# Two transformer blocks on one core: fp32 dispatch activations with one more weight tile, and another order of splits, scales and attention units around the sparse index

## The chip, the cores and the metric

The kernel runs on one core of a Trainium2 chip. Its time is that of one execution on the device, in microseconds (us); the median of several runs is compared. Engines are named as the profile names them: PE (TensorE matmul), DVE (VectorE), ACT (ScalarE), POOL (GpSimd) and SP (SyncE, which issues the weight transfers). Each engine works through its own instructions in program order and waits at semaphores for the others.

## What is computed

All is fp32, for 256 tokens of width 1024 (batch 1). The first block has convolution and neighbourhood attention, then 16 experts of which each chooses its own 32 tokens. The second has a sparse attention (top 64 keys of each query by an index score), an MLP, a latent attention and a second MLP.

```python
def ec_moe(h, w_router, w_gate, w_up, w_down):      # 16 experts, D_EXPERT 2048
    cap = EC_FACTOR * T // N_EXPERTS                # 32 tokens for each expert
    aff = softmax(h @ w_router)
    wts, tok = lax.top_k(swapaxes(aff, 1, 2), cap)
    xs = h[bidx, tok]                               # the dispatch
    hid = silu(xs @ w_gate) * (xs @ w_up)
    y = (hid @ w_down) * wts
    return zeros_like(h).at[bidx, tok].add(y)

def dsa_mixer(h, w_in, q_gain, k_gain, w_o, rel_bias, n_top):
    q, k, v, qi, ki, wi = split(h @ w_in)           # 16 query heads, one key/value head, 8 index heads
    q, k = rms_norm_2(q, q_gain), rms_norm_2(k, k_gain)
    score = sum_h(wi * relu(qi . ki))               # masked to admissible keys
    _, idx = lax.top_k(score, n_top)
    logits = q . k[idx] * A_HEAD_DIM ** -0.5 + rel_bias[t5_bucket(idx - t)]
    return softmax(logits) @ v[idx] @ w_o

x = first_block(x, ...)                             # ends in ec_moe
h = x + dsa_mixer(rms_norm_2(x)); h = h + sq_relu_mlp(rms_norm_2(h))
h = h + mla_mixer(rms_norm_2(h)); return h + sq_relu_mlp(rms_norm_2(h))
```

## The kernel before

**Weights** come in one fixed list (`loads`), issued on SP in that order. `pump` issues the next as soon as the buffer that the list names for it is free, and stops at the first that isn't; `take` and `free` follow the list on the consuming side. Expert weights use buffers of 2 MB, and for expert 0 some extra places (`RSA`, `RSB`, `RPW`, `RPN`, `RB`, `RC`) in memory that the stages before have left. `w_gu` of an expert is eight pieces of 2 MB (k = 0 to 7), `w_dn` four of 2 MB, which `parts` cuts differently for expert 0.

**Dispatch.** After wout, the normalized tokens are transposed back to token rows by ACT (`htk_out`), as a rounded half and, by POOL, the rest (`htk`, fp32r). DVE finds each expert's 32 tokens (L1008 to L1014) and PE gathers them by matmuls with a one-hot matrix (`disp`): `gather0` for expert 0, a chunk at a time between its `gate_up` steps, and `gather(g)`, twice, for the others.

**Splits.** From the second block on a product of fp32 matrices is three fp32r products, of rounded halves (`wh`, `xgh`) and remainders (`wl`, `xgl`). So each weight of 1 MB is split ahead of its use: ACT writes `wh` (L330), then DVE (L334) or POOL (L332) subtracts; `on_dve` says which. `wahead(k)` makes splits until k exist, `wnext(la)` takes one and makes `la` more. Splits 0 to 3 are the key, value and index weights (`kvi`), 4 to 7 the four query projections (`qproj(0)` to `qproj(3)`), 8 to 11 the four slots of the output projection (`dsawo`).

**The index.** After `kvi`, PE sums squares into a bank (`sps`), and DVE makes the inverse roots (`rsq`, eight small operations) of the block's norms in SBUF tiles. PE broadcasts them (`rb_`); `index_mm`, `index_acc` and `index_top` (eight rounds of MAX8 and MATCH_REPLACE8, then the mask `msk`) give the top 64 for query half 1 (256 keys) and half 0 (128 keys). `qscale(g)` makes the scales `rq` of the projected queries two projections at a time.

**The attention** has eight units (query half, group of 4 heads). `pipeline` runs it by step i: scores S(i+2), finish of unit i-2 (DVE, two operations that make hi and lo halves of the result), reciprocals and normalization of unit i (DVE, POOL), softmax of unit i+1 (DVE scales and finds the maximum, ACT exponentiates), then what `pre` lists for i, PV(i-1), the transposes T(i), and what `hooks` lists for i. Half 1 makes large units (256 keys), half 0 small ones. `qproj(3)` and `index_top(0)` (`itop`) are hooks of step -1. Slot u of dsawo needs both units of head group u and split 8 + u.

Of the kernel before, what the change touches and what calls it, by code (L numbers as in the profile page):

```python
# [63 lines left out]
def kernel(ctx: ExitStack, tc: tile.TileContext, *aps):  # L64
# [154 lines left out]
    inuse = [0] * 10  # L219
    lim = [R1, R2] + [0] * 8  # L220
    ps_ = []

    def buf(r):
        return pools[r].tile([P, 2048 if r in (RB, RC, RPN) else W1], F32, tag="w", name=nm("w"))
# [1860 lines left out]
```

## Time and profile before

| what | value |
|---|---|
| median of three runs | 1748.01 us (1747.1 to 1751.78) |
| the profiled execution | 1741.9 us, its span 1740.1 us |
| busy PE, DVE, ACT, POOL | 1356.5, 542.5, 426.0, 271.8 us of the span |
| transfers | 545.85 MB, mean 314 GB/s |
| the chain that ended last | 52% transfers, 38% PE, 5% DVE, 3% ACT |

A busy share is a mean over stages with different limits. The chain is followed back from the last instruction, at each step to what released it. Times within the kernel are counted from the start of the span.

### The profile page before, as it was taken

What the parts mean: (1) busy time and instruction counts of PE and PEld (TensorE: products, weight loads), DVE (VectorE), ACT (ScalarE), POOL (GpSimd) and SP (SyncE); (2) the same over time, 40 slices, a digit from 0 to 9 for tenths busy, and PEclk for the clock granted to TensorE, in tenths of its full rate; (3) what the DMA queues carried; (4) which work ended last, traced back from release to release, by engine and by line L of the source; (5) the groups of instructions that cost most, each with busy time, mean ns of one, the idle gap of its engine ahead of it and who ended that gap; (6) DMA issues with size and microseconds to landing.
All of it is one profiled execution on the core that took longest, in us unless ns stands there. A gap on an engine that the chain in (4) does not pass through costs nothing.

```text
span 1740.1 us, 22284 instructions
## 1 busy us (share of the span) xinstructions
PE 1356.5 (78%) x9581; PEld 873.8 (50%) x9581; DVE 542.5 (31%) x1037; ACT 426.0 (24%) x649; POOL 271.8 (16%) x124
## 2 busy tenths in 40 slices
PE   6899987666666655665666656798999999999998
PEld 3775842111111111221111111385899999889998
DVE  3885321000000000000000000278653457756434
ACT  3434510000000000000000000254554446455442
POOL 2521210000000000000000000152335221323531
PEclk9999999868778878878788787798999999999999
DMA  9649779999999999999999999972255544225450
GB/s 397 240 156 417 290 326 429 427 428 428 427 428 428 427 428 427 427 429 427 428 427 428 428 428 428 399 287 97 97 194 194 194 174 154 97 98 194 178 201 34
DMA packets 59475, 545.85 MB, mean 314 GB/s; under 512 B 5552, under 2 KB 9008, under 8 KB 26032
## 3 DMA queue, kind: packets, MB, share of 16 engines
q1 hardware_dynamic: 56400, 537.71, 74.9%
q10 hardware_dynamic: 2976, 6.72, 1.1%
q8 instruction: 75, 1.23, 0.3%
q14 instruction: 24, 0.20, 0.0%
HBM read 543.36 MB, written 1.05 MB: 313 GB/s over the span
## 4 chain that ended last, share of the span: by engine, by line
DMA 52%; PE 38%; DVE 5%; ACT 3%; issue 2%; POOL 1%; ACTq 0%; SPq 0%; DVEq 0%; POOLq 0%
DMA moe__w<-in_w_gu_dram 32%; DMA moe__w<-in_w_dn_dram 15%; PE mlp__psB L94 10%; PE mlp__psA L94 9%; PE index__psA L94 2%; DMA moe__w<-in_w_dl_dram 2%; PE mlaproj__psA L94 1%; PE mlawo__psA L94 1%; PE qkv__psA L94 1%; PE qkv__psB L94 1%; PE uproj__psA L94 1%; PE moe__psB L94 1%; DMA na__nb<-in_nab_dram 1%; PE router__psB L94 1%; PE wout__psA L94 1%
## 5 line engine op out<-in xcount | busy, mean ns | idle before, releaser
L94 PE MATMUL moe__psB<-moe__w,moe__xsT 128*32 128x512 f32 x1920 | 304.0, 767 | 191.7 <-DMA moe__w<-in_w_gu_dram 191.6
L94 PEld LDWEIGHTS moe__psB<-moe__w,moe__xsT 128*32 128x32 f32 x1920 | 58.9, 126 | 422.9 <-DMA moe__w<-in_w_gu_dram 312.3
L94 PE MATMUL moe__psB<-moe__w,moe__hT 128*32 128x512 f32 (+1 forms) x984 | 167.5, 808 | 103.1 <-DMA moe__w<-in_w_dn_dram 94.1
L1134 DVE TENSOR_TENSOR moe__hid<-moe__hid,moe__psB 128x512 f32<-128x512 f32 x15 | 10.3, 687 | 555.8 <-PE moe__psB L94 555.8
L332 POOL TENSOR_TENSOR dsaproj__wl<-moe__w,dsaproj__wh 128x1680 fp32r<-128x1680 f32 (+1 forms) x5 | 19.7, 3945 | 908.9 <-ACT dsaproj__wh L330 902.2
L94 PEld LDWEIGHTS moe__psB<-moe__w,moe__hT 128*32 128x32 f32 x984 | 38.4, 133 | 214.9 <-DMA moe__w<-in_w_dn_dram 139.7
L94 PE MATMUL mlp__psA<-mlp__hh,mlp__wl 128*128 128x256 f32 x512 | 141.3, 276 | 0.0
L94 PE MATMUL mlp__psA<-mlp__hh,mlp__wh 128*128 128x256 f32 x512 | 141.3, 276 | 0.0
L94 PE MATMUL mlp__psA<-mlp__hl,mlp__wh 128*128 128x256 f32 x512 | 141.3, 276 | 0.0
L1133 ACT ACTIVATE moe__hid<-moe__psB 128x512 f32<-128x512 f32 x15 | 9.0, 597 | 537.8 <-PE moe__psB L94 537.8
L94 PE MATMUL mlp__psB<-mlp__xgh,mlp__wh 128*128 128x256 f32 x448 | 123.8, 276 | 0.0
L94 PE MATMUL mlp__psB<-mlp__xgh,mlp__wl 128*128 128x256 f32 x448 | 123.7, 276 | 0.0
L94 PE MATMUL mlp__psB<-mlp__xgl,mlp__wh 128*128 128x256 f32 x448 | 123.7, 276 | 0.0
L330 ACT ACTIVATE mlp__wh<-mlp__w 128x2048 fp32r<-128x2048 f32 (+1 forms) x51 | 96.8, 1900 | 62.3 <-PE mlp__psA L94 48.6
L334 DVE TENSOR_TENSOR mlp__wl<-mlp__w,mlp__wh 128x2048 fp32r<-128x2048 f32 (+1 forms) x35 | 84.7, 2420 | 80.1 <-ACT mlp__wh L330 80.1
L332 POOL TENSOR_TENSOR mlp__wl<-mlp__w,mlp__wh 128x2048 fp32r<-128x2048 f32 x16 | 74.4, 4648 | 147.5 <-ACT mlp__wh L330 147.5
L94 PEld LDWEIGHTS mlp__psA<-mlp__hh,mlp__wh 128*128 128x128 f32 x512 | 96.1, 188 | 0.0
L94 PEld LDWEIGHTS mlp__psA<-mlp__hl,mlp__wh 128*128 128x128 f32 x512 | 96.1, 188 | 0.0
L94 PEld LDWEIGHTS mlp__psA<-mlp__hh,mlp__wl 128*128 128x128 f32 x512 | 96.1, 188 | 0.0
L1169 DVE COPY moe__ys<-moe__psB 128x512 f32<-128x512 f32 x15 | 10.4, 691 | 243.7 <-PE moe__psB L94 243.7
L94 PEld LDWEIGHTS mlp__psB<-mlp__xgh,mlp__wl 128*128 128x128 f32 x448 | 84.1, 188 | 0.0
L94 PEld LDWEIGHTS mlp__psB<-mlp__xgl,mlp__wh 128*128 128x128 f32 x448 | 84.1, 188 | 0.0
(602 smaller groups left out, 2508.2 us busy)
## 6 DMA issues: line engine op xcount, KB each, us to landing
moe__w<-in_w_gu_dram SPq DMA_DIRECT2D x120, 2048.0 KB, 39.1
moe__w<-in_w_dn_dram SPq DMA_DIRECT2D x57, 2048.0 KB, 39.1
mlp__w<-in_mlp_down_dram SPq DMA_DIRECT2D x28, 1024.0 KB, 7.0
mlp__w<-in_mlp_up_dram SPq DMA_DIRECT2D x20, 1024.0 KB, 4.9
qkv__w<-in_w_mod_dram SPq DMA_DIRECT2D x12, 1024.0 KB, 7.0
start__w<-in_w_mod_dram SPq DMA_DIRECT2D x8, 1024.0 KB, 13.5
mod__w<-in_w_gu_dram SPq DMA_DIRECT2D x4, 2048.0 KB, 20.8
wout__w<-in_w_gu_dram SPq DMA_DIRECT2D x4, 2048.0 KB, 8.4
```

Of the source, the lines that this page charges most:

```text
L94: nc.tensor.matmul(o, lhsT, rhs, start=start, stop=stop, skip_group_check=True)
L330: nc.scalar.activation(h[:, 0:n], f, AF.Copy)
L332: nc.gpsimd.tensor_tensor(out=l[:, 0:n], in0=f, in1=h[:, 0:n].bitcast(F32), op=ALU.subtract)
L334: nc.vector.tensor_tensor(out=l[:, 0:n], in0=f, in1=h[:, 0:n].bitcast(F32), op=ALU.subtract)
L1133: nc.scalar.activation(hid, gp, AF.Silu)
L1134: nc.vector.tensor_mul(hid, hid, up)
L1169: nc.vector.tensor_copy(ys[1], yp[1])
```

## The change

It has five parts. (1) `htk` is one fp32 tile; `gather0` and `gather` do two fp32 matmuls for a chunk where they did four fp32r ones. (2) The memory that this frees holds one more weight tile of 1 MB (`RX`): expert 0's k = 7 comes as two halves in `RB` and `RX`, and its `w_dn` is cut into five parts instead of six. (3) A new `rsq_p` keeps scales in PSUM banks. (4) Splits 7 and 9 go from POOL to DVE; 5 to 9 are made at other places of the program, 8 and 9 as `pre` of steps 2 and 3 of the attention. (5) Unit (1,3) comes before (0,0) and (0,1), `itop` is a hook of step 1, and the softmax scales the scores in their own bank.

```diff
-    parts = {0: (2, 2, 4, 2, 2, 4)}
+    parts = {0: (4, 2, 2, 4, 4)}
     for e in range(NE):
         for k in range(8):
+            if e == 0 and k == 7:
+                for h2 in range(2):
+                    ld(1, I["w_gu"][e, k * P:(k + 1) * P, 2048 * h2:2048 * h2 + 2048], 2048, ring=(RB, RX)[h2], solo=True)
+                continue
...
+    def rsq_p(pool_, v, n, tag, ps):
+        r, r1, out_ = (small(pool_, n, tag + k) for k in "012")
+        t = small(pool_, n, "rq_t")
+        a, b = ps[:, 0:n], ps[:, n:2 * n]
+        nc.vector.tensor_scalar(r.bitcast(I32), v.bitcast(I32), -0.5, 1597463007.0, ALU.mult, ALU.add)
+        nc.vector.tensor_tensor(out=a, in0=v, in1=r, op=ALU.mult)
+        nc.vector.tensor_tensor(out=t, in0=a, in1=r, op=ALU.mult)
+        nc.vector.scalar_tensor_tensor(out=b, in0=t, scalar=-10.0 / 3.0, in1=t, op0=ALU.add, op1=ALU.mult)
+        nc.vector.scalar_tensor_tensor(out=r1, in0=b, scalar=5.0, in1=r, op0=ALU.add, op1=ALU.mult)
...
-                nc.scalar.activation(htk[g][:, :, t, :], bv, AF.Copy, scale=r2[:, t:t + 1])
-                bc_ = pd.tile([P, 4, P], F32, tag="hb", name=nm("hb"), bufs=2)
-                nc.scalar.activation(bc_, bv, AF.Copy, scale=r2[:, t:t + 1])
-                nc.gpsimd.tensor_tensor(out=htk[g][:, :, 2 + t, :], in0=bc_, in1=htk[g][:, :, t, :].bitcast(F32),
-                                        op=ALU.subtract)
+                nc.scalar.activation(htk[:, 4 * g:4 * g + 4, t, :], bv, AF.Copy, scale=r2[:, t:t + 1])
...
-                    for n in range(4):
-                        mm(bs[c], htk[g][:, c, n, :], disp[n % 2], n == 0, n == 3)
+                    for n in range(2):
+                        mm(bs[c], htk[:, 4 * g + c, n, :], disp[n], n == 0, n == 1)
...
-        on_dve = {5, 8, 10, 11} | {n for n in range(12, 90) if n % 3 or 43 < n < 54}
+        on_dve = {5, 7, 8, 9, 10, 11} | {n for n in range(12, 90) if n % 3 or 43 < n < 54}
...
-                w = wnext(2 if s == 3 else 0)
+                w = wnext(1 if s == 3 else 0)
...
-        v1, pv, iv1, v2c, ep, ipv = (cols[:, 2 * i:2 * i + 2] for i in range(6))
+        v1, iv1, ep = (cols[:, 2 * i:2 * i + 2] for i in range(3))
+        vr = sps[:, 32:36]
+        vp1, pv, v2c, ipv = (sps[:, 32 + 2 * i:34 + 2 * i] for i in range(4))
...
         def qproj(u):
-            w = wnext()
+            w = wnext(0)
...
-        rk = rsq(pa, vk, 2, "rk")
-        scs[1] = index_acc(1, rl1)
+        rk = rsq_p(pa, vk, 2, "rk", kst[:, 16:20])
+        wahead(6)
+        scs[1] = index_acc(1, rl1, rb_)
...
         qproj(0)
+        wahead(7)
         index_top(1, scs[1])
...
-        scs[0] = index_acc(0, rl0)
+        scs[0] = index_acc(0, rl0, r12b)
+        wahead(8)
...
-        wahead(10)
...
+                psv = pss[par][:, 0:2 * nk].rearrange("p (a k) -> p a k", a=2)
...
-                    nc.vector.scalar_tensor_tensor(out=s[:, a, 0:nk], in0=pss[par][:, a * nk:(a + 1) * nk],
-                                                   scalar=rq[:, qt, hd:hd + 1], in1=bm[:, 2 * par + a, :],
-                                                   op0=ALU.mult, op1=ALU.add)
+                    nc.vector.scalar_tensor_tensor(out=psv[:, a, :], in0=psv[:, a, :], scalar=rq[:, qt, hd:hd + 1],
+                                                   in1=bm[:, 2 * par + a, :], op0=ALU.mult, op1=ALU.add)
...
-                  [(1, 0), (1, 1), (1, 2), (0, 0), (0, 1), (1, 3), (0, 2), (0, 3)])
+                  [(1, 0), (1, 1), (1, 2), (1, 3), (0, 0), (0, 1), (0, 2), (0, 3)])
...
-        pipeline(att, 8, "dsaatt", {-2: [lambda: qscale(0, pb)], -1: [q_last, itop], 0: [q_last2], 8: [wo.slot(2, (1,))]},
-                 {6: [wo.slot(0), x3(range(0, 3))], 7: [wo.slot(1), x3(range(3, 6))],
+        pipeline(att, 8, "dsaatt", {-2: [lambda: qscale(0, pb)], -1: [q_last], 0: [q_last2], 1: [itop], 8: [wo.slot(2, (1,))]},
+                 {2: [lambda: wahead(9)], 3: [lambda: wahead(10)], 6: [wo.slot(0), x3(range(0, 3))], 7: [wo.slot(1), x3(range(3, 6))],
```

In the text "split n" counts from 0. Three places of the program show how instructions move. The first is SP's list around the router, before (128x4096 is 2 MB, 128x2048 is 1 MB; `moe__w` is first issued when expert 0 gives a buffer back):

```order
L241 DMA wout__w_1772<-in_w_gu_dram 128x4096
L241 DMA wout__w_1774<-in_w_gu_dram 128x4096
L241 DMA wout__w_1776<-in_w_dn_dram 128x2048
L241 DMA router__w_1917<-in_w_dn_dram 128x2048
L241 DMA router__w_1919<-in_w_dn_dram 128x4096
L241 DMA router__w_1921<-in_w_dn_dram 128x2048
L241 DMA moe__w_2038<-in_w_dn_dram 128x2048
L241 DMA moe__w_2053<-in_w_dn_dram 128x4096
```

and of the change:

```order
L246 DMA wout__w_1772<-in_w_gu_dram 128x4096
L246 DMA wout__w_1774<-in_w_gu_dram 128x2048
L246 DMA router__w_1918<-in_w_gu_dram 128x2048
L246 DMA router__w_1920<-in_w_dn_dram 128x4096
L246 DMA router__w_1922<-in_w_dn_dram 128x2048
L246 DMA router__w_1924<-in_w_dn_dram 128x2048
L246 DMA router__w_1926<-in_w_dn_dram 128x4096
L246 DMA moe__w_2023<-in_w_dn_dram 128x4096
```

The two halves of `w_gu` for k = 7 now go to `RB` and to the new place, and a `w_dn` tile of 2 MB (`router__w_1926`) leaves ahead of the stop at `moe__w`: from `wout__w_1772` on 10 MB instead of 9.

The second is DVE ahead of the index, before (`moe__sqa` is the last sum of squares of the first block's result, `wl_4779` split 5, L288 and L289 the begin of `rsq`, L295 its end):

```order
L315 TENSOR_TENSOR moe__sqa_4457<-moe__sqa_4457,dsaproj__sq_4749 128x256
L334 TENSOR_TENSOR dsaproj__wl_4779<-moe__w_4522,dsaproj__wh_4778 128x2048
L1311 TENSOR_SCALAR dsaproj__cols_4835<-dsaproj__psA_4773 128x2
L1312 RECIPROCAL dsaproj__cols_4835<-dsaproj__cols_4835 128x2
L1313 TENSOR_TENSOR dsaproj__cols_4835<-dsaproj__psA_4773,dsaproj__cols_4835 128x2
...
L288 TENSOR_SCALAR dsaproj__rr_4866<-dsaproj__cols_4835 128x4
L289 TENSOR_TENSOR dsaproj__rq_t_4867<-dsaproj__rr_4866 128x4
...
L295 SCALAR_TENSOR_TENSOR dsaproj__rr_4866<-dsaproj__rq_t_4867,dsaproj__rr_4866 128x4
```

and of the change (L307 is the begin of `rsq_p`, L310 the operation with one SBUF tile as both inputs, `psA_4728` the bank `sps`, `wl_4880` split 5):

```order
L334 TENSOR_TENSOR moe__sqa_4412<-moe__sqa_4412,dsaproj__sq_4704 128x256
L1332 TENSOR_SCALAR dsaproj__cols_4783<-dsaproj__psA_4728 128x2
L1333 RECIPROCAL dsaproj__cols_4783<-dsaproj__cols_4783 128x2
L1334 TENSOR_SCALAR dsaproj__psA_4728<-dsaproj__psA_4728 128x2
L1335 TENSOR_TENSOR dsaproj__psA_4728<-dsaproj__psA_4728,dsaproj__cols_4783 128x2
...
L307 TENSOR_SCALAR dsaproj__rr_4814<-dsaproj__psA_4728 128x4
...
L310 SCALAR_TENSOR_TENSOR dsaproj__psA_4728<-dsaproj__rq_t_4817 128x4
...
L1343 TENSOR_SCALAR dsaproj__wsc_4828<-dsaproj__psA_4728 128x2
...
L314 SCALAR_TENSOR_TENSOR index__rk_4869<-index__psA_4853,index__rk_4868 128x2
L353 TENSOR_TENSOR index__wl_4880<-moe__w_4477,index__wh_4879 128x2048
```

Split 5 goes from ahead of the scales to behind the key's scale, and most of the scales' operands are in the bank.

The third is DVE in the attention, before, from the end of soft(0) to the begin of soft(1) (`sc_5032` holds the index scores of half 0, `msk_4844` is their mask):

```order
L1482 TENSOR_REDUCE dsaatt__nmx_5217<-dsaatt__ss_5216 128x2
L1395 MEMSET index__sc_5032 64x64
L1398 MAX index__m_5287<-index__sc_5032 128x8
L1399 MATCH_REPLACE index__sc_5032<-index__m_5287,index__sc_5032 128x128
...
L1400 TENSOR_SCALAR dsaproj__msk_4844<-index__sc_5032 128x128
L1254 RECIPROCAL dsaatt__sm_5210<-dsaatt__sm_5210 128x2
L1254 RECIPROCAL dsaatt__sm_5218<-dsaatt__sm_5218 128x2
L1479 SCALAR_TENSOR_TENSOR dsaatt__ss_5317<-dsaatt__psA_5200,dsaproj__rq_4840,dsaproj__t_4836 128x256 x2
```

and of the change, from the end of soft(2) to split 8 (`msk_4791` is the mask of half 0, `wl_5396` split 8):

```order
L1507 TENSOR_REDUCE dsaatt__nmx_5320<-dsaatt__psA_5236 128x2
L1417 MEMSET index__sc_4991 64x64
L1420 MAX index__m_5347<-index__sc_4991 128x8
L1421 MATCH_REPLACE index__sc_4991<-index__m_5347,index__sc_4991 128x128
...
L1422 TENSOR_SCALAR dsaproj__msk_4791<-index__sc_4991 128x128
L365 CAST index__mixah_5233<-dsaatt__psB_5327 128x2x128
L1505 SCALAR_TENSOR_TENSOR dsaatt__psA_5299<-dsaatt__psA_5299,dsaproj__rq_4788,dsaproj__t_4784 128x256 x2
L1507 TENSOR_REDUCE dsaatt__nmx_5380<-dsaatt__psA_5299 128x2
L1505 SCALAR_TENSOR_TENSOR dsaatt__psA_5300<-dsaatt__psA_5300,dsaproj__rq_4788,dsaproj__t_4784 128x256 x2
L1507 TENSOR_REDUCE dsaatt__nmx_5388<-dsaatt__psA_5300 128x2
L353 TENSOR_TENSOR dsaatt__wl_5396<-dsaproj__w_4663,dsaatt__wh_5395 128x2048
```

The eight rounds go from behind soft(0) to behind soft(2), and split 8 stands behind soft(3).

## Rows read from the trace of the kernel before

**Rows 1.** The chain that ended last, by engine and by line (the page).

```profile
DMA 52%; PE 38%; DVE 5%; ACT 3%; issue 2%; POOL 1%; ACTq 0%; SPq 0%; DVEq 0%; POOLq 0%
DMA moe__w<-in_w_gu_dram 32%; DMA moe__w<-in_w_dn_dram 15%; PE mlp__psB L94 10%; PE mlp__psA L94 9%; PE index__psA L94 2%; DMA moe__w<-in_w_dl_dram 2%; PE mlaproj__psA L94 1%; PE mlawo__psA L94 1%; PE qkv__psA L94 1%; PE qkv__psB L94 1%; PE uproj__psA L94 1%; PE moe__psB L94 1%; DMA na__nb<-in_nab_dram 1%; PE router__psB L94 1%; PE wout__psA L94 1%
```

**Rows 2.** Windows of four stretches, all engines and transfers.

```profile
core 0: us, PE busy (x) PEld busy (x) DVE busy (x) ACT busy (x) POOL busy (x), PEclk, DMA share, GB/s
221.00:229.00 8.00, 5.17 (x26) 2.87 (x26) 3.08 (x11) 0.67 (x2) 2.72 (x4) 0.57 0.04 17
241.00:300.00 59.00, 46.70 (x344) 19.87 (x336) 7.31 (x15) 5.49 (x8) 0.00 (x0) 0.97 1.01 428
1205.00:1224.00 19.00, 15.67 (x101) 10.04 (x97) 16.63 (x54) 12.55 (x45) 8.48 (x10) 0.86 0.00 1
1224.00:1250.00 26.00, 25.80 (x211) 23.68 (x210) 15.26 (x29) 11.49 (x18) 9.11 (x5) 0.97 0.22 82
```

**Rows 3.** When SP issued transfers (start us, us, what, count).

```profile
208.85 1.81 SPq L241 DMA_DIRECT2D router__w<-in_w_dn_dram  x3
229.48 2.72 SPq L241 DMA_DIRECT2D moe__w<-in_w_dn_dram  x2
```

**Rows 4.** Timeline of DVE and POOL at the end of the router.

```profile
222.58 0.66 DVE L1014 CAST router__idf<-router__idu 16x32 f32<-16x32 uint32 x1
...
218.28 4.92 POOL L979 TENSOR_TENSOR router__htk<-router__hb,router__htk 128x512 fp32r<-128x512 f32 x4 [0.45 <-ACT router__hb L978]
```

**Rows 5.** PE's gathers and gate_up, and the expert transfers' landing (the page).

```profile
258.67 3.92 PE L94 MATMUL router__psA<-router__disp,router__htk 128*128 128x512 f32 x16
...
280.58 1.92 PE L94 MATMUL moe__psB<-moe__w,moe__xsT 128*32 128x512 f32 x16 [0.22 <-DMA moe__w<-in_w_gu_dram]
...
moe__w<-in_w_gu_dram SPq DMA_DIRECT2D x120, 2048.0 KB, 39.1
```

**Rows 6.** POOL, DVE and PE ahead of the index.

```profile
1147.92 4.58 POOL L332 TENSOR_TENSOR dsaproj__wl<-moe__w,dsaproj__wh 128x2048 fp32r<-128x2048 f32 x1 [3.44 <-PE dsaproj__psB L94]
...
1149.68 4.97 DVE L334 TENSOR_TENSOR dsaproj__wl<-moe__w,dsaproj__wh 128x2048 fp32r<-128x2048 f32 x1 [3.18 <-ACT dsaproj__wh L330]
...
1154.95 0.16 DVE L1313 TENSOR_TENSOR dsaproj__cols<-dsaproj__psA,dsaproj__cols 128x2 f32<-128x2 f32 x1
...
1157.14 2.00 PE L94 MATMUL index__psA<-cst,dsaproj__rr 128*128 128x128 f32 x8 [3.52 <-DVE dsaproj__rr L295]
```

**Rows 7.** The chain of waits from the index on (start us, us, what).

```profile
1160.98 5.67 PE index__psA L94 x48
...
1182.70 4.38 DVE dsaatt__rqq L288
...
1189.81 8.05 PE index__psA L94 x48
...
1224.28 6.11 PE dsawo__psA L94 x48
```

**Rows 8.** Timeline of POOL and DVE in the index.

```profile
1169.83 4.59 POOL L332 TENSOR_TENSOR index__wl<-dsaproj__w,index__wh 128x2048 fp32r<-128x2048 f32 x1 [0.84 <-ACT index__wh L330]
1182.54 4.51 POOL L332 TENSOR_TENSOR index__wl<-dsaproj__w,index__wh 128x2048 fp32r<-128x2048 f32 x1 [8.12 <-ACT index__wh L330]
...
1172.62 1.95 DVE L1400 TENSOR_SCALAR dsaproj__msk<-index__sc 128x256 fp32r<-128x256 f32 x1
```

**Rows 9.** Window of one pair of exponentials on ACT.

```profile
1190.41:1191.51 1.10, 1.10 (x7) 1.10 (x7) 1.07 (x3) 1.09 (x4) 0.00 (x0) 0.50 1.03 417
```

**Rows 10.** Windows of itop, of soft(2), of a small unit's finish and softmax.

```profile
1191.84:1197.95 6.11, 6.11 (x42) 5.91 (x41) 5.53 (x29) 1.15 (x5) 0.00 (x0) 0.76 0.35 142
1205.27:1208.59 3.32, 1.56 (x12) 1.16 (x14) 3.25 (x10) 1.09 (x4) 2.04 (x2) 0.98 0.00 0
1212.16:1215.10 2.94, 2.94 (x22) 1.96 (x24) 2.84 (x10) 2.62 (x10) 1.18 (x2) 1.00 0.02 6
```

**Rows 11.** DVE's half of split 10, after its wait.

```profile
1229.45 2.29 DVE L334 TENSOR_TENSOR dsawo__wl<-dsaproj__w,dsawo__wh 128x2048 fp32r<-128x2048 f32 x1 [3.09 <-ACT dsawo__wh L330]
```

More of the change, by code (lines that the diff above doesn't have):

```diff
@@ L218 @@
             slots.append(r)
[L219 to L220 removed]
+    inuse = [0] * 11
+    lim = [R1, R2] + [0] * 9
     ps_ = []
     def buf(r):
[L224 removed]
+        return pools[r].tile([P, 2048 if r in (RB, RC, RPN, RX) else W1], F32, tag="xs0" if r == RX else "w",
+                             name=nm("w"))
     bufs_ = {}
@@ L296, in rsq @@
         return r
+    def rsq_p(pool_, v, n, tag, ps):
[7 more added lines that the diff above has]
+        nc.vector.scalar_tensor_tensor(out=r1, in0=b, scalar=5.0, in1=r, op0=ALU.add, op1=ALU.mult)
+        nc.vector.scalar_tensor_tensor(out=a, in0=v, scalar=-27.0 / 1024.0, in1=r1, op0=ALU.mult, op1=ALU.mult)
+        nc.vector.tensor_tensor(out=b, in0=a, in1=r1, op=ALU.mult)
+        nc.vector.scalar_tensor_tensor(out=out_, in0=b, scalar=0.5625, in1=r1, op0=ALU.add, op1=ALU.mult)
+        return out_
     def sumsq(pool_, ps, src, n, c, rhs, first, last, w=1, o=0, sqb=3):
@@ L959 @@
         p2 = p2s.enter_context(pool("p2"))
-        htk = [p2.tile([P, 4, 4, P], F32R, tag=f"xs{g}", name=nm("htk"), bufs=1) for g in range(2)]
+        pools[RX] = p2
+        lim[RX] = 1
+        pump()
+        htk = p2.tile([P, 8, 2, P], F32, tag="xs1", name=nm("htk"), bufs=1)
         xsT = []
@@ L1050, in gather @@
                 for c in range(4):
-                    for n in range(4):
-                        mm(bs[c], htk[g][:, c, n, :], disp[n % 2], n == 0, n == 3)
+                    for n in range(2):
+                        mm(bs[c], htk[:, 4 * g + c, n, :], disp[n], n == 0, n == 1)
                 return bs
@@ L1066, in gate_up @@
                 xs = xsT[k // 4][:, k % 4, e * CAP:(e + 1) * CAP] if e else xs0[k]
-                w = take()
+                two = e == 0 and k == 7
                 for i, o in enumerate(gu):
+                    if i == 0 or two:
+                        w = take()
+                    w_ = w if two else w[:, 2048 * i:2048 * i + 2048]
                     for j in range(4):
-                        mm(o[32 * j:32 * j + 32, :], xs, w[:, 2048 * i + j * 512:2048 * i + (j + 1) * 512], k == 0,
-                           k == 7)
-                free()
+                        mm(o[32 * j:32 * j + 32, :], xs, w_[:, j * 512:(j + 1) * 512], k == 0, k == 7)
+                    if i or two:
+                        free()
             gu0 = (bank("B"), bank("B"))
@@ L1312 @@
         nc.vector.reciprocal(iv1, v1)
+        nc.vector.tensor_scalar(vp1, sps[:, 0:2], 1.0 / D, EPS, ALU.mult, ALU.add)
         nc.vector.tensor_tensor(out=v2c, in0=sps[:, 2:4], in1=iv1, op=ALU.mult)
@@ L1354, in qscale @@
                 nc.tensor.transpose(qc[:, t * 8:(t + 1) * 8], rw[:, t * P:(t + 1) * P], ident[0:8, 0:8])
-            vq = small(pool_, 16, "vq")
+            vq = qc[:, 32:48]
             for t in range(2):
```

27 lines of the change are left out of this document (13 added, 14 removed).

## Prediction

> **What bounds the kernel now.** I read the chain that ended last first [rows 1]: transfers hold 52% of it, nearly all of that expert weights (32% and 15%), so the first block ends when its last weights land and PE follows; the rest is PE, the two MLPs above all. The windows [rows 2] show the hole in the expert stream: from 221 to 229 the queues move 17 GB/s, from 241 on 428 GB/s, with PE at 46.70 of 59 us. The issues [rows 3] say why: the last transfer ahead of the hole leaves at 210.66 (three of them, 208.85 + 1.81), the next at 229.48, when expert 0's first matmuls give a buffer back. A byte moved into the hole is a byte less at the end.
>
> Around the sparse index PE leads the chain [rows 6, 7], with two stops: 3.52 us before the broadcast of the scales, and the stretch in which DVE's first operation of the q scale takes 4.38 us. In the attention the chain passes between DVE, ACT and PE from unit to unit, until dsawo's first slot starts on PE at 1224.28; from there PE is busy 25.80 of 26.00 us [rows 2], up to mlp0.
>
> The sum is made in this execution's time (1741.9 us, its span 1740.1). The median of the three runs shown is 1748.01, 6.1 higher, which I add at the end.
>
> **Dispatch and the extra tile.** One tile of 1.049 MB more leaves ahead of the hole and is missing behind it: 1.049 / 0.428 = 2.45 us. The 7 MB (7.34 in decimal) issued from about 209 on need 7.34 / 0.428 = 17.2 us, to about 226.5; that is before 229.5, so they fit. The extra tile waits for the memory that mix leaves when wout's matmuls end, near 209; only transfers stand behind it on SP, and a bubble there is taken out of the hole. Four POOL subtractions go, the last of which ends at 223.20 (218.28 + 4.92); DVE's cast of the chosen indices, for which PE waits, ends right behind it, after 0.66 us for 16x32 elements [rows 4]. DVE's small operations without POOL took 0.16 to 0.2 [rows 6], so I take 0.45. The transfer that restarts the stream is 2 MB instead of 1 MB, so the queue doesn't run dry once more before the second: 0.3. Together **-3.2 us**. Bounds: 0, if the tile comes late or the stream is held later, and -4.
>
> What could hold it later is the gather in plain fp32. Its 16 instructions took 3.92 us [rows 5]. The nearest fp32 row is gate_up, 16 instructions in 1.92 us with four column groups side by side: 4 x 1.92 = 7.7 us for a gather, +3.8 us, twice. Before, PE waits for a weight transfer again at 280.58; until then it works off tiles that had landed, 1.92 us each against 2.097 / 0.428 = 4.9 us of transfer. So it is level two or three tiles later than before, and the queues stay fed as long as buffers come back in time: a transfer is issued a median of 39.1 us before it lands [rows 5]. I cost it at nothing; without that cover it is up to 3 us.
>
> **Scales and splits ahead of the index.** Before, DVE does split 5 first [rows 6]: it starts at 1149.68, is held by POOL's split (1147.92 + 4.58 = 1152.50) and ends at 1154.65; thirteen small operations later, 0.19 us each, PE starts the broadcast at 1157.14 and needs 2.00 us for 8 matmuls. After, split 5 stands behind that chain, which begins when the sums are there, near 1149.5. Nine operations lead to 1151.3. The tenth (L310 of the new code) reads one SBUF tile twice while POOL is in its split; I let it wait until 1152.5. It, four more and the three that read the broadcast's bank make 8 x 0.2: PE starts near 1154.1. As it stood 0.6 us instead of 3.52, I expect the full clock: 0.96 us for the broadcast, 1.0 for the index matmuls behind it. qproj(0) starts at 1156.1 instead of 1161.0 [rows 7], **-4.9**.
>
> Two rules of the Trainium skill bear on this, and the sum needs neither. "SBUF — State Buffer", section "Who interferes with whom": a DVE operation with at most one SBUF input, outside the two-port modes, does not contend with GpSimd; one with two SBUF inputs contends with GpSimd's reads. The trace agrees in split 5 (4.97 us beside POOL, 2.29 without it [rows 6, 11]); by this rule the tenth operation waits, without it the broadcast comes 0.9 us sooner. "Perfetto Trace Analysis", section "Optimizing Scalar/DVE Operations", speaks against the change: about 125 ns of access overhead for DVE on PSUM, 60 on SBUF. As an estimate from that page the some 33 operations on the path would cost 33 x 0.065 = 2.1 us more. The rows don't bear it out: L1313 reads the bank and took 0.16 [rows 6].
>
> qproj(0) ends at 1161.8, qproj(1) follows. qproj(2) needs POOL's split: before, POOL's split behind qproj(0) (which ended at 1166.65) ended at 1169.83 + 4.59 = 1174.42 [rows 8], 7.8 us later; so 1161.8 + 7.8 = 1169.6 against 1173.7, and S(0) at 1176.3 instead of 1180.3, **-4.0**. DVE's own line sets the q scale: index_top(1) ends as before, since split 5 now stands where the chain stood; its mask, held for 1.95 us beside POOL [rows 8], takes some 0.4, so split 7 there ends at 1178.7 against split 8's 1180.5; then copy, transposes and eleven operations, 3.0. Before, they were held beside POOL's split 9 (1182.54 + 4.51 = 1187.05 [rows 8]). rq(0) is ready at 1181.7 instead of 1188.7, **-7.0**.
>
> In place of that wait another begins. The softmax now works inside the score bank, so the bank comes free when ACT's exponentials end, 0.9 + 0.7 of DVE and 1.10 of ACT [rows 9] behind rq(0): qproj(3) starts at 1184.5 against 1189.81, **-5.3**. It took 8.05 us against 5.67 for qproj(0) [rows 7], and I leave that. S(2) waits the same way, and rq(1) is ready at 1201.5 instead of 1205.4, **-3.9**. Up to here the change wins.
>
> **Attention.** Now three things that lay beside other work stand in DVE's line between rq(1) and dsawo's first slot, as the order shows. itop takes 6.1 us, in which PE, busy with qproj(3), lost nothing [rows 10]. After, DVE is idle from about 1189.3 to 1198.5 and does itop behind soft(2), while S(4), PV(1) and T(2) queue on PE behind the mask. Splits 8 and 9 stand behind soft(3) and soft(4), and their ACT half behind that unit's exponentials, so DVE waits: split 10 shows this pattern already before, 3.09 us of waiting for ACT's copy, then 2.29 [rows 11]. So 5.4 us for the one, 5.2 for the other (smaller exponentials); before, split 8 was done at 1180.5, split 9 on POOL.
>
> DVE's line from 1201.5: soft(2) with its reciprocals 3.3 [rows 10]; itop 6.1; the finish of a unit (hi/lo) 0.9 and soft(3), a large unit, 3.2; split 8 with its wait 5.4; a small unit, finish and softmax, 2.94 [rows 10]; split 9 with its wait 5.2; two small units 5.9; the finish of (0,0) 0.9. The sum is 33.8: at 1235.3 dsawo's slot 0, which needs (1,0) and (0,0), starts, against 1224.28: **+11.0**. (Unit (0,0) is now the fifth, not the fourth.) Slot 1 needs (0,1), now the sixth, whose finish stands on DVE behind the last softmax (to 1237.4), split 10 with its wait (1242.6) and the update of x (1.3): ready at 1244.8, while PE is through with slot 0 and one more unit at 1242.4, so 2.4 more. dsawo ends **+13.4**, and mlp0 and all behind it shift with it. Bounds: the first slot at a lower clock after so thin a stretch, up to 8.05 - 5.67 = +2.4 on top; the other end is +5, if both waits behind exponentials are covered (2 x 3.0) and PE takes 2 of itop back.
>
> Sum: -3.2 + 13.4 = +10.2: 1741.9 + 10.2 = 1752.1 for such an execution, 1748.0 + 10.2 = **1758.2** as a median.
>
> **The rivals.** *Other side: DVE doesn't set the tail.* If PE sets the units' pace, itop and the splits fall into slack, the gain at rq(1) stays, and the sum is -3.9 - 3.2 = -7.1: 1740.9. It decides if DVE's line has 15 us of slack from 1205 to 1224. For it: PE is busy 15.67 of 19 us there; against: DVE is busy 16.63 [rows 2]. Chance 0.17. *Half of it*: itop is exposed, the waits before the splits are not: +5 - 3.2 = +1.8, 1749.8. For it: ACT is busy 12.55 of the 19, so its copies could come early. Chance 0.18. *The extra tile does nothing*: the wait for mix's memory or the longer gathers use up what the hole gives: 1761.4. The gathers speak for it, the queue's depth against. Chance 0.15. My forecast has the remaining 0.50.
>
> **Numbers.** About 0.3%, 5.2 us, is what a measurement of this kernel tells from no change: 1742.8 to 1753.2. The forecast and the third rival are slower than that, 0.65, less 0.03 for the forecast's low end: slower 0.62. The first rival and as little of the second, faster 0.18; same 0.20. The range goes from the first rival to the idle tile with the lower clock added: 1741 to 1765 (1761.4 + 2.4 = 1763.8). That of the likeliest alone is 1754 to 1763.
>
> **What would show it.** Right: the stream ends about 3 us sooner; in times less those 3, the broadcast at 1154, rq(0) 7 and qproj(3) 5 us ahead; DVE idle 9 us during qproj(3); MAX8 of 128x128 behind soft(2), with PE idle 6 to 7 us before S(4); DVE idle some 3 us before each of two splits; slot 0 some 11 us late. Wrong: no such idle time on PE among the units, a split without its wait, or a stream that ends where it did.

## The result, and the profile after

The change makes the kernel slower: a median of 1759.52 us (1758.9 to 1763.35, five runs) against 1747.18 (1746.73 to 1751.78, five runs). The medians are 12.3 us apart; the ratio is 1.0066 [1.0042, 1.009], which is 11.5 us (7.3 to 15.7). The profiled executions are 17.0 apart (1758.9 and 1741.9), since that of before lies 5.3 below its median, and below all five runs.

The chain that ended last, the page of after, by engine; it answers to [rows 1]:

```profile
DMA 51%; PE 36%; DVE 6%; ACT 3%; issue 2%; POOL 1%; ACTq 0%; SPq 0%; DVEq 0%; POOLq 0%
```

The windows of after, with the columns of [rows 2]: the hole, the stretch behind it, the two stretches around dsawo's start before, and the whole line from rq(1) to dsawo after:

```profile
core 0: us, PE busy (x) PEld busy (x) DVE busy (x) ACT busy (x) POOL busy (x), PEclk, DMA share, GB/s
221.00:229.00 8.00, 5.92 (x26) 2.88 (x26) 2.34 (x11) 0.00 (x0) 0.52 (x2) 0.50 0.92 387
241.00:300.00 59.00, 53.19 (x363) 21.07 (x356) 8.00 (x16) 6.20 (x9) 0.00 (x0) 1.00 1.00 427
1205.00:1224.00 19.00, 9.69 (x49) 5.86 (x48) 15.09 (x49) 7.55 (x23) 3.74 (x4) 0.68 0.00 1
1224.00:1250.00 26.00, 22.83 (x131) 17.13 (x130) 18.04 (x41) 13.90 (x38) 5.06 (x9) 0.71 0.21 82
...
1202.30:1236.00 33.70, 20.94 (x100) 12.50 (x96) 26.46 (x76) 15.11 (x45) 8.47 (x10) 0.64 0.16 60
```

The hole is filled: 387 GB/s where 17 flowed. But PE, busy 15.67 of 19 us from 1205 on before, is now busy 9.69; dsawo and mlp0 have moved out of these windows.

The dispatch in the timelines of SP, DVE and PE, against [rows 3 to 5]:

```profile
209.13 0.33 SPq L246 DMA_DIRECT2D router__w<-in_w_gu_dram  x1
209.50 2.80 SPq L246 DMA_DIRECT2D router__w<-in_w_dn_dram  x4
229.19 0.33 SPq L246 DMA_DIRECT2D moe__w<-in_w_dn_dram  x1
...
222.33 0.17 DVE L1032 CAST router__idf<-router__idu 16x32 f32<-16x32 uint32 x1
...
246.22 7.13 PE L94 MATMUL router__psA<-router__disp,router__htk 128*128 128x512 f32 x16
```

Five transfers leave ahead of the stop at `moe__w`, where there were three; the cast takes 0.17 us instead of 0.66, and a gather 7.13 instead of 3.92.

The index and the attention in the timelines of ACT, DVE, POOL and PE, in the order of time, against [rows 6 to 8] and [rows 10, 11]; in brackets the idle time ahead and what ended it:

```profile
1144.42 4.55 POOL L351 TENSOR_TENSOR dsaproj__wl<-moe__w,dsaproj__wh 128x2048 fp32r<-128x2048 f32 x1 [3.44 <-PE dsaproj__psB L94]
...
1147.55 1.44 DVE L310 SCALAR_TENSOR_TENSOR dsaproj__psA<-dsaproj__rq_t 128x4 f32<-128x4 f32 x1
...
1150.32 1.16 PE L94 MATMUL index__psA<-cst,dsaproj__rr 128*128 128x128 f32 x8 [0.20 <-DVE dsaproj__wsc L1343]
...
1160.49 0.38 ACT L1445 ACTIVATE dsaproj__r1b<-index__psA 128x256 f32<-128x256 f32 x1 [2.97 <-DVE index__sc L1412]
...
1162.13 3.70 ACT L349 ACTIVATE index__wh<-dsaproj__w 128x2048 fp32r<-128x2048 f32 x2
...
1164.11 4.53 POOL L351 TENSOR_TENSOR index__wl<-dsaproj__w,index__wh 128x2048 fp32r<-128x2048 f32 x1 [15.14 <-ACT index__wh L349]
...
1168.69 0.58 PE L94 MATMUL index__psA<-moe__xgh,index__wl 128*128 128x256 f32 x1 [2.95 <-POOL index__wl L351]
...
1184.10 1.28 ACT L1509 ACT_TABLE_LOAD   x1 [5.92 <-DVE dsaatt__nmx L1507]
...
1199.09 0.41 DVE L1373 COPY index__rw<-index__psB 8x256 f32<-8x256 f32 x1 [8.27 <-PE index__psB L94]
...
1211.57 0.23 DVE L1422 TENSOR_SCALAR dsaproj__msk<-index__sc 128x128 fp32r<-128x128 f32 x1
...
1211.85 0.80 PE L94 MATMUL dsaatt__psA<-dsaproj__msk,dsaproj__idr 128*128 128x256 f32 x2 [4.30 <-DVE dsaproj__msk L1422]
...
1218.96 2.29 DVE L353 TENSOR_TENSOR dsaatt__wl<-dsaproj__w,dsaatt__wh 128x2048 fp32r<-128x2048 f32 x1 [2.95 <-ACT dsaatt__wh L349]
...
1227.15 2.29 DVE L353 TENSOR_TENSOR dsaatt__wl<-dsaproj__w,dsaatt__wh 128x2048 fp32r<-128x2048 f32 x1 [2.73 <-ACT dsaatt__wh L349]
...
1237.25 0.56 PE L94 MATMUL dsawo__psA<-index__mixah,dsaatt__wh 128*128 128x256 f32 x1
```

The broadcast starts 6.8 us sooner than in [rows 6], and the first slot of dsawo 13.0 later than in [rows 7]. Between them DVE is idle 8.27 us, then does the eight rounds up to the mask while PE waits 4.30 for it, then waits twice for ACT's half of a split.

And the chain of waits (start, us, what), at the last expert weights, at qproj(2), qproj(3), dsawo's second slot and mlp0:

```profile
1093.25 22.48 DMA moe__w<-in_w_dl_dram
...
1168.69 8.20 PE index__psA L94 x46
...
1186.47 8.07 PE index__psA L94 x48
...
1246.91 5.61 PE dsawo__psA L94 x47
...
1266.25 23.84 PE mlp__psB L94 x208
```

The stream ends at 1115.73; before it ended at 1119.24 (its chain piece, 1091.99 + 27.25). mlp0 starts at 1266.25 against 1251.37, 14.9 later. The other 2.1 of the 17.0 come behind that: mlp0, whose instructions are the same, is 2.7 longer (173.0 against 170.3), and 0.6 come back later. Windows of mlp0 in which PE never stops, before and, in a fence of its own, after:

```profile
1375.00:1400.00 25.00, 25.00 (x223) 25.00 (x222) 10.01 (x7) 9.92 (x8) 9.04 (x2) 1.00 0.49 185
```

```profile
1390.00:1416.80 26.80, 26.80 (x230) 26.80 (x229) 9.77 (x7) 10.29 (x9) 9.21 (x2) 1.00 0.49 183
```

A matmul comes every 0.112 us before (25.00 / 223) and every 0.117 after (26.80 / 230), at a granted clock of 1.00 in both. In the chains of all profiles, those of the experiments below included, nearly every group of 48 matmuls of the two MLPs takes either 5.44 or 5.65 us: none takes 5.65 in before, e3, e7 and e8, 8 do in after, 29 in e5 and in e12, 33 in e1. So I put these 2.1 us to the spread of executions and not to the change. What sets the pace isn't known.

### The profile page after: what moved, and what is told of

Read it like the earlier page. It is cut to its first block, busy times and chain, and to the rows that moved or that the text cites. A ratio compares the mean times of both kernels' runs of the same rounds, so it can differ in the third digit from the quotient of the medians.

```text
span 1757.1 us, 22282 instructions
## 1 busy us (share of the span) xinstructions
PE 1363.5 (78%) x9581; PEld 880.2 (50%) x9581; DVE 540.4 (31%) x1040; ACT 422.4 (24%) x646; POOL 253.2 (14%) x117
## 4 chain that ended last, share of the span: by engine, by line
DMA 51%; PE 36%; DVE 6%; ACT 3%; issue 2%; POOL 1%; ACTq 0%; SPq 0%; DVEq 0%; POOLq 0%
DMA moe__w<-in_w_gu_dram 31%; DMA moe__w<-in_w_dn_dram 14%; PE mlp__psB L94 10%; PE mlp__psA L94 9%; PE mlaproj__psA L94 1%; PE mlawo__psA L94 1%; PE moe__psB L94 1%; DMA moe__w<-in_w_dl_dram 1%; PE qkv__psA L94 1%; PE qkv__psB L94 1%; PE uproj__psA L94 1%; DMA na__nb<-in_nab_dram 1%; PE router__psA L94 1%; PE index__psA L94 1%; PE router__psB L94 1%
## 5 line engine op out<-in xcount | busy, mean ns | idle before, releaser
L94 PE MATMUL moe__psB<-moe__w,moe__xsT 128*32 128x512 f32 x1920 | 298.4, 755 | 198.5 <-DMA moe__w<-in_w_gu_dram 198.3
L94 PE MATMUL moe__psB<-moe__w,moe__hT 128*32 128x512 f32 (+1 forms) x976 | 159.0, 782 | 98.6 <-DMA moe__w<-in_w_dn_dram 88.8
L94 PEld LDWEIGHTS mlp__psB<-mlp__xgh,mlp__wh 128*128 128x128 f32 x448 | 84.1, 188 | 0.0
```

The source lines that it names most:

```text
L94: nc.tensor.matmul(o, lhsT, rhs, start=start, stop=stop, skip_group_check=True)
```

## The experiments

Three theories stood behind the expectations (before, after, and e1 to e12 are the kernels of the table). *Theory 1*, that of the prediction: DVE's line sets the tail, and itop and splits 8 and 9, put into it between rq(1) and dsawo, are the loss. *Theory 2*: the softmax in its bank holds PSUM, so PE waits for ACT. *Theory 3*: thinner work on PE costs granted clock.

Each experiment was timed in five rounds against before on one chip. The three batches (e1 to e4, e5 to e8, e9 to e12) ran on three chips, so kernels of different batches are compared by their ratios to before. To read the middle part without the stream, all profiles are counted from one event that every kernel has: PE's matmuls that sum the keys' squares (`index__psA<-cst,dsaproj__sqk`), at 1153.02 before and 1149.51 after, in both 33.78 us behind the stream's end. The columns rq(0) and rq(1) are the ends of the operations that write the q scales, mlp0 its start in the chain of waits.

| kernel | median us | ratio to before | to rq(0) | to rq(1) | to mlp0 |
|---|---|---|---|---|---|
| before | 1747.18 | 1 | 35.7 | 52.4 | 98.4 |
| after | 1759.52 | 1.0066 [1.0042, 1.009] | 32.7 | 52.8 | 116.7 |
| e1, itop back | 1755.25 | 1.0045 [1.0022, 1.0069] | 32.7 | 52.8 | 111.0 |
| e2, splits back | 1751.81 | 1.0022 [1.0001, 1.0044] | 30.0 | 49.4 | 104.7 |
| e3, both back | 1745.81 | 0.9991 [0.9972, 1.0011] | 31.7 | 52.8 | 101.0 |
| e4, dispatch and tile alone | 1742.38 | 0.9969 [0.9951, 0.9987] | 35.7 | 52.6 | 99.8 |
| e5, softmax through SBUF | 1755.4 | 1.0046 [1.0024, 1.0069] | 32.7 | 48.9 | 111.0 |
| e6, ACT freed | 1756.73 | 1.0057 [1.0039, 1.0075] | 28.3 | 48.8 | 112.8 |
| e7, all back | 1736.26 | 0.9956 [0.9935, 0.9976] | 28.3 | 50.5 | 95.3 |
| e8, scales alone | 1743.49 | 0.9988 [0.9961, 1.0014] | 36.9 | 53.2 | 98.5 |
| e9, e7 with the new order | 1741.48 | 0.9969 [0.9949, 0.9989] | 28.3 | 50.5 | 98.7 |
| e10, e7, split 9 on POOL | 1739.15 | 0.9966 [0.9944, 0.9987] | 28.3 | 51.4 | 96.3 |
| e11, fp32 dispatch, no tile | 1744.87 | 0.9993 [0.9971, 1.0015] | 35.9 | 52.7 | 98.7 |
| e12, e7 with the bank | 1744.33 | 0.9992 [0.997, 1.0015] | 28.3 | 49.4 | 98.5 |

Before's medians in the three batches were 1746.61, 1746.27 and 1744.47.

**itop and the splits (e1 to e3, on after).** The new lines of each, in turn; e2 and e3 also lose the entries 2 and 3 of `pre`:

```diff
-  -1: [q_last], 0: [q_last2], 1: [itop],
+  -1: [q_last, itop], 0: [q_last2],
...
+  -1: [lambda: wahead(10), q_last], 0: [q_last2], 1: [itop],
...
+  -1: [itop, lambda: wahead(10), q_last], 0: [q_last2],
```

> The changed kernel with itop as the last hook of step -1 again, where DVE is idle for some 8 us while PE runs qproj(3). Theory 1 (DVE's line: itop and the splits 8 and 9 stand between rq(1) and dsawo's first slot, each with its own price): the 6.1 us of itop leave that line, 5.8 of them arrive at the end, 1753.7 us, and PE no longer stops 4.3 us for the mask. Theory 2 (the banks: the softmax in the score bank holds qproj(3) and every S(i) until ACT's exponentials end, and that sets the pace): within 1 us of the changed kernel, 1759. Theory 3 (the clock: PE at the lower clock in the thin stretch costs more than the waits themselves): more than its price, 1751 or less.

> The changed kernel with splits 8 and 9 made at step -1 ahead of qproj(3), behind soft(0) on DVE and its exponentials on ACT, and none in steps 2 and 3; itop stays behind soft(2). Theory 1: both splits with their waits for ACT (5.4 and 5.2 us) leave DVE's line between rq(1) and slot 0, and 9.8 of these 10.6 us arrive, 1749.7 us. Theory 2: 1758 to 1759. Theory 3: 1748 or less.

> The changed kernel with itop and then splits 8 and 9 at step -1 ahead of qproj(3). They are some 11 us of DVE in an idle stretch of some 8, so rq(1) comes about 2 us later. Theory 1: -13.5 us, 1746.0. Theory 2: 1757. Theory 3: 1744 or less.

All three came within some 2 us of theory 1's number. On the way to mlp0 e1 gains 5.7 us, e2 12.1, e3 15.7 of the 18.4 that the change adds. But 3.4 of e2's 12.1 were there at rq(1) already and aren't the price of splits in DVE's line: its qproj(2) ran at the full clock (shown with e6), and its qproj(3) took 7.3 us instead of 8.1. From rq(1) to mlp0 itop is worth 5.7 us, the splits 8.7 and both 15.7. By the ratios e3 lies clear of after and e2 all but; e1's interval overlaps after's, so the price of itop alone rests on the profile. In e1 DVE's idle time ahead of `index__rw` falls from 8.27 to 3.9, and PE's wait for the mask is gone; in e2 the wait for the mask stays (4.3).

**The dispatch (e4, e11, on before).** e4 is the diff up to `gate_up` (L1082), with `rsq_p` defined but not used; e11 takes of it only the fp32 `htk`, `disp0`, `disp` and the two matmuls for a chunk, with the old list of loads.

```diff
+        pools[RX] = p2
+        lim[RX] = 1
...
+                    for n in range(2):
+                        mm(bs[c], htk[:, 4 * g + c, n, :], disp[n], n == 0, n == 1)
```

> The kernel before with the dispatch in fp32 and the one more weight tile alone; scales, splits and attention as before. The stream ends 3.5 us sooner in the profile of the change; if nothing behind it takes that back: 1747.2 - 3.5 = 1743.7. If the stretch behind the stream was bound by something else (weights of the second block, loaded behind the stream): 1746 to 1747.

> The kernel before with the dispatch in plain fp32 alone: no extra tile, weights in the list and the places of before. The gathers took 7.13 us each instead of 3.92 in the profile of the change, and DVE's cast came 0.5 us sooner. If the queues stay fed, as I costed it: -0.5, 1746.0, and the gain of 4.2 us of the tile kernel is the tile's. If the gathers hold the stream: +2 to +3, 1749. If the freed POOL and ACT work is the gain: 1743.

e4 is faster than before by 5.4 us (2.3 to 8.6); e11 can't be told from before, nor, since their intervals overlap, from e4. The chain of e11 at the last weights:

```profile
1091.17 28.96 DMA moe__w<-in_w_dl_dram
```

It ends at 1120.13. Over the nine profiles with the tile whose chain shows it the stream ends at 1116.4 on average (1115.2 to 1117.1), over the three without it (before, e8, e11) at 1119.6. So it is the tile that moves the stream's end, by 3.2 us. The longer gathers, together with the freed work of POOL and ACT, leave it within 0.9 us of before's 1119.24.

**The bank of the scores (e5, on after).** The softmax writes to SBUF again:

```diff
-                    nc.vector.scalar_tensor_tensor(out=psv[:, a, :], in0=psv[:, a, :], scalar=rq[:, qt, hd:hd + 1],
+                    nc.vector.scalar_tensor_tensor(out=s[:, a, 0:nk], in0=pss[par][:, a * nk:(a + 1) * nk],
...
-                nc.vector.tensor_reduce(nmx, psv, axis=AX.X, op=ALU.max, negate=True)
+                nc.vector.tensor_reduce(nmx, s[:, :, 0:nk], axis=AX.X, op=ALU.max, negate=True)
```

> The changed kernel with the softmax of the sparse attention through an SBUF tile again, so that DVE's scaling frees the score bank and ACT's exponentials wait for DVE alone. In the profile of the change qproj(3) waited 4.95 us for the exponentials, 1.28 of it a table load that now stood behind DVE's maximum. Theory 1 (DVE's line after rq(1) sets the end, but rq(1) itself comes behind qproj(3)): qproj(3) 3 to 4 us sooner and the end with it, -4.0, 1755.5. If the banks hold the later units too (theory 2): -8 or more, 1751. If neither matters: 1759.

From the list of PE's waits after (total, times, longest) qproj(3)'s, and in a fence of its own the timelines of ACT and PE in e5:

```profile
PE index__psA L94 <- ACT dsaatt__ss L1509: 5.0, 1, 5.0
```

```profile
1179.43 1.28 ACT L1509 ACT_TABLE_LOAD   x1
...
1184.53 0.35 PE L94 MATMUL index__psA<-moe__xgh,index__wh 128*128 128x256 f32 x1 [1.78 <-DVE dsaatt__ss L1504]
```

qproj(3) waits 1.78 us for DVE, where it waited 4.95 for ACT after, and the load of the exponential's table needs no wait and lies ahead; after, it waited 5.92 for DVE's maximum and stood in the way (1184.10). Counted from the common event rq(1) comes 3.9 us sooner than after, and mlp0 5.8. The median is theory 1's number, though by the ratios e5 and after aren't told apart. In the profile the 3.9 up to rq(1) are theory 1's, and the 1.9 behind it are left for theory 2.

**The copy that waits for a bank (e6, on after).** DVE's index sum reads the copy of the scale in SBUF, as before, and not the bank `rb_`:

```diff
-        scs[1] = index_acc(1, rl1, rb_)
+        scs[1] = index_acc(1, rl1, r12b)
```

> The changed kernel with index_acc(1) reading the scales' SBUF copy r12b instead of the bank rb_. In the profile of the change ACT stood 2.97 us before its copy of the bank's other half until DVE's last read of the bank, and with it the ACT half of split 6, so that qproj(2) waited 2.95 us and then ran at half clock (8.20 us instead of 5.67). If that wait was due to the shared bank: qproj(2) without the stop, 4 to 5 us sooner, the end -4.0, 1755.5. If ACT was held by the buffers of index_acc's inputs instead: at most -1, 1758.5.

The timelines of ACT and PE in e6:

```profile
1157.72 0.38 ACT L1445 ACTIVATE dsaproj__r1b<-index__psA 128x256 f32<-128x256 f32 x1
...
1166.38 0.38 PE L94 MATMUL index__psA<-moe__xgh,index__wl 128*128 128x256 f32 x1 [0.35 <-POOL index__wl L351]
```

ACT's copy doesn't wait, and PE's wait for split 6 falls from 2.95 to 0.35; rq(0) comes 4.5 us sooner and mlp0 4.0. In the medians e6 and after can't be told apart (their intervals overlap by most of their width), so this is shown in profiles alone, but there in ten: the copy waits 2.97 us in the five kernels in which DVE reads the bank (after, e1, e2, e3, e5) and not at all in the five of the change in which it doesn't (e6, e7, e9, e10, e12). Some of the 4.5 is clock. The windows of qproj(2) after, and, in a fence of its own, of e2, which has the same 3.0 us wait ahead of it:

```profile
1168.69:1176.88 8.19, 8.19 (x47) 8.06 (x48) 5.71 (x12) 0.00 (x0) 0.00 (x0) 0.65 0.09 18
```

```profile
1168.11:1173.70 5.59, 5.58 (x47) 5.40 (x48) 5.24 (x12) 0.05 (x1) 0.00 (x0) 1.00 0.00 0
```

At a granted clock of 0.65 (in part at the lower of the two levels) the same matmuls take 8.2 us, at 1.00 5.6. So theory 3 is worth 2.6 us there. Up to this point e2 is the same program as after, with the same wait and the full clock, so it parts the two: S(0) starts 28.3 us behind the common event after, 25.6 in e2 and 22.9 in e6, so 2.7 are the clock's and 2.6 the wait's. At rq(0), which in e6 stands behind DVE's own line, they are 2.7 and 1.8. The same wait came with either clock: qproj(2) took 8.2 us in after, e1 and e5, 7.1 in e3 and 5.5 in e2.

**What is left of the change when its losses go (e7; e9, e10 and e12 on e7).** e7 is e3 with e5's and e6's edits and the old order of units. It keeps the fp32 dispatch and the tile, the scales in banks, the places of splits 5 to 7, and splits 7 and 9 on DVE. e9 has the new order, e10 gives split 9 back to POOL, e12 leaves the softmax in the bank.

```diff
-                  [(1, 0), (1, 1), (1, 2), (1, 3), (0, 0), (0, 1), (0, 2), (0, 3)])
+                  [(1, 0), (1, 1), (1, 2), (0, 0), (0, 1), (1, 3), (0, 2), (0, 3)])
...
-        on_dve = {5, 7, 8, 9, 10, 11} | {n for n in range(12, 90) if n % 3 or 43 < n < 54}
+        on_dve = {5, 7, 8, 10, 11} | {n for n in range(12, 90) if n % 3 or 43 < n < 54}
```

> The change with all that theory 1 holds against it undone: itop and splits 8 and 9 ahead of qproj(3), the softmax through SBUF, index_acc(1) from r12b, and the units in the order of before. Kept: the dispatch with its tile, the scales in the banks, split 7 and 9 on DVE, splits 5 to 7 at their new places. Theory 1: the stream's 3.5 us and some 2.5 us of the index stay, 1746.6 - 6.0 = 1740.6. If the new scales and splits around the index are worth nothing by themselves: as the tile alone, 1742.5 to 1743.

> The kernel with all undone that theory 1 holds against the change (median 1736.3), but with the units in the order of the change, (1,3) ahead of (0,0) and (0,1). dsawo's slots 0 and 1 then wait for the fifth and the sixth unit instead of the fourth and the sixth. Theory 1: slot 0 one small unit later, of which PE fills a part: +2.0, 1738.3. If the order is free: 1736.3. If it costs two full units: +6, 1742.

> The same kernel (median 1736.3, units in the order of before) with split 9 on POOL, where it runs beside itop's MAX8 and MATCH_REPLACE8. In the profile of the 1736.3 kernel PE waited 4.76 us for the normalization of unit 0, whose reciprocals stood on DVE behind itop and both splits (4.49 us). Theory 1: 2.2 us less on DVE and the same at the end, 1734. If POOL's split holds itop or is itself late for the normalization: 1738 or more.

> The 1736.3 kernel with the softmax in the score bank, as in the change. Theory 1: qproj(3) waits for the exponentials of unit 0 and the table load, +1.9 to +3, 1738.7. Theory 2 (the banks set the pace of all units): +8 or more, 1744. If ACT's exponentials were never late: 1736.3.

The first pair of lines is part of e7's edit (e9 takes it back), the second turns e7 into e10. e7 beats both kernels: 7.7 us under before, and 4.3 under what was expected. Of the 7.7 the tile alone, e4, had 5.4; the ratios of e7 and e4 overlap, so what the new scales and splits give beyond the tile, 4.5 us up to mlp0, is shown in the profile alone. The new order costs e9 some 2.3 us by the two ratios (0.0013, whose intervals overlap) and 3.4 up to mlp0; PE waits 2.9 us in all for the finished units, where e7 has 0.2:

```profile
1228.11 0.38 PE L94 MATMUL dsawo__psA<-index__mixah,index__wh 128*128 128x256 f32 x1 [2.16 <-DVE index__mixah L365]
```

e10 missed; the timelines of DVE and POOL show why:

```profile
1186.34 3.57 DVE L1422 TENSOR_SCALAR dsaproj__msk<-index__sc 128x128 fp32r<-128x128 f32 x1
...
1185.30 4.52 POOL L351 TENSOR_TENSOR index__wl<-dsaproj__w,index__wh 128x2048 fp32r<-128x2048 f32 x1 [19.72 <-ACT index__wh L349]
```

The mask, 0.23 us in e7, is held beside POOL's split until it ends: DVE saves the 2.3 us of a split and pays 3.3 there, and rq(1) comes 0.9 later. e10 isn't better than e7; by the ratios it is 1.7 us worse, by the intervals not told apart. e12 missed too: 3.2 us more than e7 up to mlp0, near theory 1's number, but 6.3 by the ratios, between the theories; the spread of both leaves 1 to 12. The list of PE's waits (total, times, longest) in e12 has what e7's has not:

```profile
PE index__psA L94 <- DVE index__sc L1421: 5.0, 1, 5.0
PE dsaatt__psA L94 <- ACT dsaatt__ss L1509: 3.4, 3, 1.2
```

The first is qproj(3)'s wait; the list puts it down to itop, which runs on DVE beside it, but the exponentials, whose table load waited 6.6 us for the maximum, stand just ahead. The second is that of the scores for the exponentials. The 3.2 up to mlp0 doesn't come by theory 1's path: qproj(3) starts 3.2 us later than in e7, but rq(1), which stands on DVE behind both splits, comes 1.1 sooner, and the loss is made behind it, where e12 needs 49.2 us to mlp0 and e7 44.8. There the second line belongs, which is theory 2's.

**The scales alone (e8, on before).** `rsq_p` and its operands in the banks, all else as before; line numbers differ (L305 is L310 of the change).

```diff
-            rqq = rsq(pool_, vq, 16, "rqq")
+            rqq = rsq_p(pool_, vq, 16, "rqq", qc[:, 64:96])
```

> The kernel before with only the scales' operands moved to the banks; splits, order and attention as before, so that POOL's split 9 still runs beside the q scale. If operands in a bank keep DVE clear of POOL: the 4.38 us of the first operation become 0.2, rq(0) and qproj(3) come 4 us sooner, 1746.6 - 4 = 1742.6. If one operation with two SBUF inputs (L310 of the new code, which took 1.45 us beside POOL in the profile of the change) is held as the first was: the wait moves to it, and the time is the same within 1 us.

It can't be told from before. The timelines of DVE and POOL:

```profile
1184.86 0.17 DVE L302 TENSOR_SCALAR dsaatt__rqq<-dsaatt__psB 128x16 int32<-128x16 int32 x1
1185.49 3.61 DVE L305 SCALAR_TENSOR_TENSOR dsaatt__psB<-dsaatt__rq_t 128x16 f32<-128x16 f32 x1
...
1184.55 4.51 POOL L346 TENSOR_TENSOR index__wl<-dsaproj__w,index__wh 128x2048 fp32r<-128x2048 f32 x1 [8.13 <-ACT index__wh L344]
```

The first operation, held for 4.38 us before [rows 7], takes 0.17 from the bank; the fourth, which reads one SBUF tile as both inputs, is held for 3.61 instead. The bank alone moves the wait by three operations. What removes it is split 9's move away from there: after, that operation takes 0.18.

## Why the prediction was right, and where it was not

**The dispatch** (-3.2): right in size and cause. -3.5 in the two profiles, -3.2 over twelve, and e11 shows that it is the tile. The terms of 0.45 for the cast and 0.3 for the restart no run shows by themselves: e11 has the cast at 0.17 us, and its stream ends no sooner than before's. The gather was forecast at 7.7 us and took 7.13, at no cost that shows.

**The broadcast and qproj(0)** (-4.9): right. Counted without the stream's 3.5 the broadcast starts at 1153.8 (forecast 1154.1), qproj(0) at 1156.0 (1156.1), and L310 was held until POOL's split ended, at the very 1152.5 of the forecast. One edit that the five parts don't name belongs here: the rounding of an identity (`idr`), 2.36 us on POOL right behind that split before, is done by ACT after (0.30 us), so nothing of POOL follows the split. L310, and L305 in e8, agree with the rule on two inputs of the Trainium skill, "SBUF — State Buffer", "Who interferes with whom", if one tile read twice counts as two. The mask in e10 and the first operation in [rows 7] read one SBUF tile and were held too; that the rule allows in a two-port mode only, and no run shows the mode. The rule of the Trainium skill, "Perfetto Trace Analysis", "Optimizing Scalar/DVE Operations", on PSUM's access overhead was rightly left aside: the operations on the bank took 0.15 to 0.17 us (L1334 to L1337), as L1313 did before [rows 6], and L1333, in SBUF alone, 0.17.

**S(0)** (-4.0): the step that failed. "qproj(2) needs POOL's split ... 7.8 us later" took for granted that ACT's half of split 6 comes as soon after qproj(0) as the split made behind qproj(0) did before. After, POOL's split ended 10.5 us behind qproj(0) (1168.64), in e6 7.9. ACT stood in the copy `r1b`, which waited 2.97 us for DVE's last read of the other half of the bank `rb_`, because the change lets DVE read that bank. Then qproj(2) ran in part at the lower clock. Without the stream S(0) came 1.0 us later than before, not 4.0 sooner: 2.6 of the difference to e6 are the wait's and 2.7 the clock's, by e2. e6, with that read taken away, gives the forecast back: S(0) -4.3, rq(0) at 28.3 from the common event against 35.7, -7.5 (forecast -7.0), and rq(1) -3.6 (forecast -3.9), where after shows -3.0 and +0.4.

**qproj(3)** (-5.3): without the stream it started 0.2 us later than before. Most of the miss is rq(0)'s, handed on; the step itself was mis-sized. The hold of the bank was seen, the table load behind DVE's maximum (1.28 us) was not: from rq(0) to qproj(3) after needs 1186.47 - 1182.24 = 4.2 us, where 2.8 were forecast.

**The attention** (+11.0 to the first slot, +13.4 to mlp0): the line of DVE was right. From rq(1) to the first slot it was forecast at 33.8 us and took 34.95 (1237.25 - 1202.3), with itop behind soft(2), the mask's wait, and waits of 2.95 and 2.73 us ahead of both splits (3.09 in [rows 11]). From there to mlp0 29.0 us against 27.1 before, +1.9, forecast +2.4. But what lay ahead of it didn't bring its -3.9, so without the stream the first slot came 16.5 us late and not 11.0, and the stretch up to mlp0 grew by 18.4 us, not by 13.4. In e6 it grew by 14.4. Of the signs, PE's stop for the mask was 4.30 us and not 6 to 7.

So -3.2 + 13.4 = +10.2 stood for what is -3.5 + 18.4 = +14.9 in the two profiles, and the medians' +12.3 lies between. The mechanism was right from rq(1) on; that the sum came so close with its S(0) step 5 us off was in part luck, since the medians happen to lie less far apart than the profiles. e1 to e3 confirm the chosen mechanism against the rival that DVE has slack, and against "half of it": the splits, not only itop, are exposed. The rival of the idle tile falls by the stream's end.

Open stays why qproj(2) got the lower clock in some kernels and not in others behind the same wait, how much of S(0)'s loss the medians would show (e6), and what the softmax in the bank costs in them (e12).

## What to carry to other kernels

An engine's idle time is a place, not an amount: under qproj(3) itop filled time in which DVE was idle, and behind soft(2) the same work cost 5.7 us. Work that needs a second engine's half (here ACT's copy ahead of a split) must be issued well before the line that sets the end, or that line pays for both. When an operand moves into a bank, list everyone who touches that bank: here a reader of its other half waited 3 us, and the operation that was to be freed only handed its wait on.
